# Turning the query packs in other steps of a decoder block, and masking the mixing weights on GpSimd

## The chip, the cores and the metric

The kernel runs on one core of one Trainium2 chip. The metric is the device time of the program in microseconds, the median of three runs. The profile is of one execution of its own; its times are given in us from the first instruction.

## The reference

The block takes `x` (512 positions of 1024 channels) through a normalisation and one input projection, whose columns are cut into `a_u`, `a_v`, attention `q`, `k`, `v`, indexer `q`, `k` and weights, and two gates. Branch A mixes positions in chunks of 128 by a lower-triangular matrix for each of eight groups; branch B is sparse attention with a partial rotary embedding on the first 32 channels of each head. Then come projections, gates, and a SwiGLU layer.

```python
h = rms_norm(x, norm1_g) * (1.0 + scale1) + shift1
a_u, a_v, q, k, v, qi, ki, wi, g_a, g_b = jnp.split(h @ w_in, split_points, axis=-1)

# chunked_gmlp(gelu(a_u), gelu(a_v), ...)
v = layer_norm(v, ln_g, ln_b).reshape(bsz, n, CHUNK, A_GROUPS, A_GROUP_DIM)
mask = jnp.tril(jnp.ones((CHUNK, CHUNK), dtype=w_s.dtype))
mixed = jnp.einsum('gts,bnsgc->bntgc', w_s * mask, v) + b_s.T[None, None, :, :, None]
y_a = u * mixed.reshape(bsz, s, A_WIDTH)

# partial_rope(q, pos, ROT_DIM) on 32 of 128 channels of each head
rot = jnp.concatenate([x1 * cos - x2 * sin, x2 * cos + x1 * sin], axis=-1)

merged = sigmoid(g_a) * (y_a @ w_proj_a) + sigmoid(g_b) * (y_b @ w_proj_b)
x = x + gate1 * (merged @ w_out)
```

## The kernel before

Every large product is made of three matmuls, high times high, high times low and low times high, where a float32 operand is split into a rounded high part and the rest, its low part. Weights come in chunks of 128x1024, in the order of a list. For each chunk the SyncE queue issues the load, ScalarE copies the high part (line 163), and VectorE or GpSimd subtracts it from the raw chunk to get the low part (line 167). `get` prepares a chunk two chunks ahead of the one whose matmuls are issued (24 of them, lines 107 to 109). All engines run their instructions in the order in which the program was written, so what is written earlier on an engine's queue stands ahead, waiting or not. The buffers of high and low parts are three each.

Three stages matter here. In the stage of `a_v` the loop over `s` goes through fourteen products (two halves of seven, a Strassen scheme), and the table `VT` says what else is issued at each step: weight splits, and steps of the packs below. Then `opt_b` runs over the eight chunks of `a_u`, and after them over pairs of chunks of gate A and projection A in turn, 24 chunks in all. I number them 0 to 23. Before each of them `au_tasks` is called, which counts the same number as its step `s`; after each `au_post` is called. The low parts of chunks 0 to 4 are VectorE's, those of chunks 5 to 23 nearly all GpSimd's.

- `ln_v` and `ln_v2` normalise `gelu(a_v)`: statistics in the last a_v steps and step 0, a power on GpSimd for the reciprocal root, then two operations of 128x1024 for each of four blocks on VectorE (lines 1139 and 1140), two blocks in step 1 and two in step 2.
- `mix_mm` (line 1153) multiplies `vg` with the masked mixing weights `wmT`: product 0 after chunk 3, 1 and 2 after chunk 4, 3 to 7 after chunks 5 to 9. `mix_ev` evacuates a product in the step that follows: VectorE adds the bias `bsb` and multiplies by `u`, ScalarE makes the high part of `y`, VectorE the low part. Chunks 10 and 11, of projection A, are the first to read `y`.
- `ws_mask` multiplies `wmT` by a triangle of ones, `triu`, which SyncE loads early from a constant; `load_ws` and `load_bs` load `wmT` and `bsb` from GpSimd's queue. In step 2 the program holds, in this order, the q4 turn, the mask, the bias load, and then the norms.
- `run_bg` puts operations of the search for the largest 128 scores (lines 856 and 860) between the others on VectorE.

The rotary embedding of `q` and `k` goes through packs (class `Packed`). `gather` writes the 32 rotated rows of each head to DRAM, `fetch` reads them back into a tile of 128 partitions, twice with the halves exchanged, `turn` does three VectorE operations with the table `tab_q`, `put` writes the result to DRAM, and `scatter` reads it back to its place. All these transfers are issued from GpSimd: `gather`, `fetch` and `scatter` are four issues each for a query pack, `put` one. There are three packs: `k`, `q0` (heads 0 to 3) and `q4` (heads 4 to 7). The first consumer of a turned query is `at_split` in step 20. All packs are fetched into the tile `S2_4`, which is needed for a part of `y` later. The bias tile `bsb` has the place of the table, `G3`, so its load waits for the last turn that reads the table.

Of the kernel before, what the change touches and what calls it, by code (L numbers as in the profile page):

```python
# [9 lines left out]
F32 = mybir.dt.float32  # L10
# [3 lines left out]
OP = mybir.AluOpType  # L14
AX = mybir.AxisListType

S = 512
# [40 lines left out]
@with_exitstack  # L58
def block_kernel(ctx: ExitStack, tc: tile.TileContext, x, x_t, w_in,
                 gmlp_ln_g, gmlp_ln_b, gmlp_w_s, gmlp_b_s, w_proj_a, w_proj_b,  # L60
                 w_out, w_ffn_in, w_ffn_out, final_norm_g, small, consts, c_row, w_shsc, out):
    nc = tc.nc
    T, V, A, P, SY = nc.tensor, nc.vector, nc.scalar, nc.gpsimd, nc.sync
    ctx.enter_context(tc.manual_schedule())
# [6 lines left out]
    x, out = x[0], out[0]  # L71
# [14 lines left out]
    def at_line(pool, tag, dims, dt, name, off=0):  # L86

        n = math.prod(dims)
        pad = 256 if tag == "E6" else (256 - HOME[tag]) % 256 or 192 if tag in HOME else 0
        t = pool.tile([128, n + pad // 4], dt, name=name, tag=tag, bufs=1)  # L90
        o = (off - HOME.get(tag, 0)) % 256 // 4
        letters = "abcd"[:len(dims)]
        return t[:, o:o + n].rearrange(f"p ({' '.join(letters)}) -> p {' '.join(letters)}",
                                       **dict(zip(letters[1:], dims[1:])))
# [505 lines left out]
    for kt in range(8):  # L600
        hi, lo = chunk[W1[kt]]
        V.tensor_sub(hT[kt][1], hfs[kt], f(hT[kt][0]))
        ensure(W1M[FIRST[kt]])
        if kt < 7:
            ensure(W1[kt + 1])
        wl = [(hi[:, 0, m * 128:(m + 1) * 128], lo[:, 0, m * 128:(m + 1) * 128]) for m in range(6)]
        hh, hl = hT[kt]
        kw = dict(skip_group_check=True)
        for m in range(6):
            T.matmul(outs[m], wl[m][0], hh, start=kt == 0, stop=False, **kw)  # L610
        for m in range(6):
            T.matmul(outs[m], wl[m][1], hh, start=False, stop=False, **kw)
        for m in range(6):
            T.matmul(outs[m], wl[m][0], hl, start=False, stop=kt == 7, **kw)
        if kt < 7:
            if kt < 5:
                low_w1(kt + 1)
            else:
                stream[W1[kt + 1]]["do"]()
            for k in (kt + 2,) if 0 < kt < 4 else (6, 7) if kt == 4 else ():  # L620
                row_scale(k)
            run_chain(kt == 1)
            ensure(W1M[BEHIND[kt]])
            stage_E(kt + 1)
        else:
            ensure(W_Q[0][1])
        if kt in (1, 2):
            A.activation(csb[:, (kt - 1) * 512:kt * 512], pc[:, (kt - 1) * 512:kt * 512], AF.Copy)
        if kt == 3:
            sines()  # L630
        if kt == 4:
            triu = mid.tile([128, 2, 128], F32, name="triu", tag="ql", bufs=2)[:, 0]
            SY.dma_start(triu, consts)
            for b in range(4):
                table_dma("q", b)
            for b in range(1, 4):
                table_dma("i", b)
            table_dma("i", 0)
            table_spread()
# [21 lines left out]
    class Packed:  # L661
# [14 lines left out]
                    P.dma_start(self.rows_of(0, 2 * self.rows, j, h), t[16 * h:16 * h + 16])  # L676

        def fetch(self):
            t = at_line(base, "S2_4", (2, S), F32, "pk")
            self.a, self.b = t[:, 0], t[:, 1]  # L680
            for o, flip in ((self.a, 0), (self.b, 1)):
                for h in range(2):
                    k = self.rows * (h ^ flip)
                    src = self.d[0][k:k + self.rows]
                    if self.rows < 64:
                        src = src[None].to_broadcast([2, 32, S])
                    P.dma_start(o[64 * h:64 * h + 64], src)
# [333 lines left out]
    late = {}  # L1021
# [8 lines left out]
        P.dma_start(late["wmT"], gmlp_w_s)  # L1030

    def load_bs():
        late["bsb"] = mid.tile([128, 8, 128], F32, name="bsb", tag="G3", bufs=1)
        P.dma_start(late["bsb"], bass.AP(tensor=gmlp_b_s.tensor, offset=gmlp_b_s.offset,
                                         ap=[[0, 128], [128, 8], [1, 128]]))

    def ws_mask():
        V.tensor_tensor(late["wmT"], late["wmT"], triu[:, None, :].to_broadcast([128, 8, 128]), op=OP.mult)

    for _ in range(16):  # L1040
        bg.append((1.4, topk_max))
# [34 lines left out]
    def av_add(k, op, src):  # L1076
        op(AV[k], AV[k], kept[src])

    pq0, pkk, pq4 = packs["q0"], packs["k"], Packed("q4", qf[2:])
    VT = {0: [lambda: av_sum(0, "T2"), lambda: av_w(0, "T2"), lambda: av_issue(1, "T1", "B11"), pq0.gather],  # L1080
          1: [lambda: av_w(0, "B21")],
          2: [lambda: av_w(0, "T3"), lambda: av_sum(0, "T4"), lambda: av_acc(1, "T1")],
          3: [lambda: av_w(0, "B22"), pkk.turn, pq4.gather],
          4: [lambda: av_w(0, "T4"), lambda: av_issue(1, "B21", "T3", "B22")],
          5: [lambda: av_w(1, "B11"), pkk.put],
          6: [lambda: av_w(1, "T1"), lambda: av_acc(1, "T3"), lambda: issue(W_AU[0][0])],
          7: [lambda: av_sum(1, "T2"), lambda: av_w(1, "T2"), pkk.scatter, pq0.fetch],
          8: [lambda: av_w(1, "B21")],
          9: [lambda: av_w(1, "T3"), lambda: av_sum(1, "T4"), pq0.turn],
          10: [lambda: av_w(1, "B22"), load_ln],  # L1090
          11: [lambda: av_w(1, "T4"), lambda: issue(W_AU[0][1]), lambda: ln_v(0, 0), pq0.put],
          12: [lambda: ensure(W_AU[0][0]), lambda: ln_v(1, 0), lambda: ln_v(2, 0), load_ws, pq0.scatter, pq4.fetch],
          13: [lambda: ensure(W_AU[0][1]), lambda: ln_v(3, 0), lambda: k_b(0)]}

    def av_post(g, p):
        if p == 0:
# [68 lines left out]
    austep = [0, 0]  # L1165
    AT = {3: [0], 4: [1, 2], 5: [3], 6: [4], 7: [5], 8: [6], 9: [7]}

    def au_post():
        for m in AT.get(austep[1], []):
            mix_mm(m)  # L1170
        austep[1] += 1

    def au_tasks():
        s = austep[0]
        austep[0] += 1
        if s == 0:
            k_b(1)
        if s == 2:
            pq4.turn()
            ws_mask()  # L1180
            load_bs()
        if s in (4, 5):
            (pq4.put, pq4.scatter)[s - 4]()
        if s == 0:
            for tk in range(4):
                ln_v(tk, 1)
            rstd(rva, mva[:, :, 1], 4, 1.0)
            run_bg(0.8)
        elif s == 1:
            ln_v2(0)  # L1190
            ln_v2(1)
        elif s == 2:
            ln_v2(2)
            ln_v2(3)
        for m in AT.get(s - 1, []):
            mix_ev(m)
        if s > 2:
            run_bg(1.6 if s < 8 else 2.0)
        if s in (20, 21):
            at_split(s - 20)  # L1200
# [976 lines left out]
    for tk in range(2):  # L2177
# [26 lines left out]


_INS = ["x", "x_t", "w_in", "gmlp_ln_g", "gmlp_ln_b", "gmlp_w_s", "gmlp_b_s",
        "w_proj_a", "w_proj_b", "w_out", "w_ffn_in", "w_ffn_out", "final_norm_g", "small", "consts",
        "c_row", "w_shsc"]
_OUTS = [((1, 512, 1024), "float32")]


def _constants():
    import numpy as np
    return np.triu(np.ones((128, 128))).astype(np.float32)


def _freqs():
# [44 lines left out]
```

## Time and profile before

| what | value |
|---|---|
| median of 3 runs | 790.44 us (789.35 to 790.44) |
| the profiled execution's own time | 789.18 us |
| its span, first to last instruction | 787.5 us |
| mean granted clock of TensorE | 0.994 |
| TensorE busy | 771.8 us, 98% |
| VectorE busy | 667.9 us, 85% |
| ScalarE busy | 440.0 us, 56% |
| GpSimd busy | 191.7 us, 24% |

PE is TensorE's matmuls, PEld its weight loads, DVE VectorE, ACT ScalarE, POOL GpSimd and SP SyncE. A row of a timeline gives the start, the duration and, in brackets, how long the engine was idle before it and what ended that. Instructions overlap a little at their ends, so the distance between two starts says more of the cost than a duration. A matmul's duration has the length of the pipeline in it. The granted clock is the share of full speed (2.4 GHz) that TensorE had; its lower level is 1.2 GHz.

### The profile page before, as it was taken

The page shows a single profiled execution, that of the slowest core. Times are in us where ns is not written, and L with a number is a line of the kernel's source. Part 1 is how long each engine was busy: PE and PEld are TensorE (multiplying, and loading weights), DVE is VectorE, ACT ScalarE, POOL GpSimd, SP SyncE. Part 2 cuts the span into 40 slices and gives each one's busy share as a digit, 9 for nine tenths or more (in the row PEclk, how much of TensorE's full clock was granted, in tenths as well). Part 3 has the DMA queues.
Part 4 walks back from the last instruction along what each step waited for, and adds up shares of the span by engine and source line. Part 5 has one row for each costly group of instructions (what it writes and reads, how often), then busy time and mean ns, then how long its engine had stood idle before and what let it go on. Part 6 is the DMA issues. An engine that isn't in the chain of part 4 may idle for free.

```text
span 787.5 us, 12682 instructions
## 1 busy us (share of the span) xinstructions
PE 771.8 (98%) x4723; PEld 692.4 (88%) x4723; DVE 667.9 (85%) x1115; ACT 440.0 (56%) x775; POOL 191.7 (24%) x268
## 2 busy tenths in 40 slices
PE   8999999989999999999999999999999999999996
PEld 6899899867888888998888899999999999888885
DVE  7889778998898559987697878989999888998886
ACT  6665557522232336666536577655566666676653
POOL 4872212323354411100010000313131223000002
PEclk9999999999999999999999999999999999999998
DMA  9967655732346558717681603889897977567662
GB/s 352 415 188 191 157 149 144 241 121 93 107 161 211 187 192 218 208 56 271 213 263 28 214 1 104 246 240 302 237 283 218 278 216 194 161 195 203 214 216 107
DMA packets 54656, 153.49 MB, mean 195 GB/s; under 512 B 15585, under 2 KB 16353, under 8 KB 54594
## 3 DMA queue, kind: packets, MB, share of 16 engines
q1 hardware_dynamic: 41696, 115.40, 43.6%
q0 software_dynamic: 12320, 36.32, 19.2%
q8 instruction: 37, 0.61, 0.3%
q10 hardware_dynamic: 578, 0.95, 0.3%
q14 instruction: 25, 0.20, 0.1%
HBM read 146.35 MB, written 28.71 MB: 222 GB/s over the span
## 4 chain that ended last, share of the span: by engine, by line
PE 76%; DVE 2%; issue 0%; ACT 0%; POOLq 0%; POOL 0%; DVEq 0%
PE R L107 8%; PE R L109 8%; PE R L108 8%; PE pb L108 7%; PE pb L107 7%; PE pb L109 6%; PE pfo L109 4%; PE pfo L107 4%; PE pfo L108 4%; PE pgb L107 2%; PE pgb L108 2%; PE pgb L109 2%; PE po L107 2%; PE po L108 2%; PE po L109 2%; PE pf L107 1%
## 5 line engine op out<-in xcount | busy, mean ns | idle before, releaser
L163 ACT ACTIVATE hi<-raw 128x1024 fp32r<-128x1024 f32 (+4 forms) x98 | 98.7, 1010 | 88.6 <-PE pb L108 29.5
L167 DVE TENSOR_TENSOR lo<-raw,hi 128x1024 fp32r<-128x1024 f32 (+2 forms) x71 | 82.9, 1168 | 22.3 <-ACT hi L163 22.1
L107 PE MATMUL pb<-h,hi 128*128 128x512 f32 (+1 forms) x192 | 74.1, 386 | 0.0
L108 PE MATMUL pb<-h,hi 128*128 128x512 f32 (+1 forms) x192 | 73.5, 383 | 0.0
L109 PE MATMUL pb<-h,lo 128*128 128x512 f32 (+1 forms) x192 | 73.3, 382 | 0.0
L167 POOL TENSOR_TENSOR lo<-raw,hi 128x1024 fp32r<-128x1024 f32 x19 | 46.0, 2425 | 64.1 <-ACT hi L163 60.1
L108 PE MATMUL pfo<-lo,za 128*128 128x512 f32 (+1 forms) x144 | 55.2, 383 | 0.0
L109 PE MATMUL pfo<-hi,za 128*128 128x512 f32 (+1 forms) x144 | 55.2, 383 | 0.0
L107 PE MATMUL pfo<-hi,za 128*128 128x512 f32 (+1 forms) x144 | 55.2, 383 | 0.0
L254 DVE CUSTOM_DVE_ANT_0 mraw<-mraw,csb,cols 128x1024 f32<-128x1024 f32 x27 | 37.8, 1399 | 18.6 <-DMA mraw<-in_w_shsc_dram 18.5
L387 POOL COPY sm<-sm 128x1 f32<-128x1 f32 x36 | 26.9, 751 | 94.1 <-ACT sm L386 94.1
L107 PE MATMUL R<-tb,hi 128*128 128x256 f32 x160 | 44.2, 276 | 0.0
L108 PE MATMUL R<-tb,hi 128*128 128x256 f32 x160 | 44.2, 276 | 0.0
L109 PE MATMUL R<-tb,lo 128*128 128x256 f32 x160 | 44.2, 276 | 0.0
L107 PE MATMUL R<-tb,sx 128*128 128x256 f32 x160 | 44.2, 276 | 0.0
L108 PE MATMUL R<-tb,sx 128*128 128x256 f32 x160 | 44.2, 276 | 0.0
L109 PE MATMUL R<-tb,sx 128*128 128x256 f32 x160 | 44.2, 276 | 0.0
L109 PEld LDWEIGHTS pb<-h,lo 128*128 128x128 f32 x192 | 36.3, 189 | 6.6 <-DVE lo L167 0.4
L107 PEld LDWEIGHTS pb<-h,hi 128*128 128x128 f32 x192 | 36.4, 190 | 6.0
L108 PEld LDWEIGHTS pb<-h,hi 128*128 128x128 f32 x192 | 36.4, 189 | 6.0
L367 POOL DMA_DIRECT2D wsum<-in_w_ffn_out_dram x24 | 19.6, 823 | 66.6 <-DMA wsum<-wsum 39.2
L108 PEld LDWEIGHTS pfo<-lo,za 128*128 128x128 f32 x144 | 27.1, 188 | 5.3
(419 smaller groups left out, 2666.9 us busy)
## 6 DMA issues: line engine op xcount, KB each, us to landing
raw<-in_w_ffn_in_dram SPq DMA_DIRECT2D x44, 512.0 KB
raw<-in_w_in_dram SPq DMA_DIRECT2D x38, 512.0 KB
wsum<-in_w_ffn_out_dram POOLq DMA_DIRECT2D x30, 512.0 KB, 7.1
mraw<-in_w_shsc_dram SPq DMA_DIRECT2D x27, 512.0 KB
raw<-wsum SPq DMA_DIRECT2D x20, 512.0 KB
s<-in_w_shsc_dram SPq DMA_DIRECT2D x14, 512.0 KB
raw<-in_w_ffn_out_dram SPq DMA_DIRECT2D x13, 512.0 KB
wsum<-wsum POOLq DMA_DIRECT2D x10, 512.0 KB, 5.8
```

The lines of the kernel that those rows point to most:

```text
L107: T.matmul(o, wh, rh, start=start, stop=False, **kw)
L108: T.matmul(o, wh, rlo, start=False, stop=False, **kw)
L109: T.matmul(o, wlo, rh, start=False, stop=stop, **kw)
L163: A.activation(hi[:, :m], e["raw"][:, :m], AF.Copy)
L167: e["lo"].tensor_sub(lo[:, :m], e["raw"][:, :m], f(hi[:, :m]))
L254: V.tensor_tensor_reduce(out=raw[:, c], in0=raw[:, c], in1=(csb if s > 1 else pc)[:, c], scale=scale, scalar=sums.pop(0), op0=OP.mult, op1 ...
L367: P.dma_start(wsum_at(n, c), src, max_dma_last_dim=4096, accum_op=OP.add)
L387: P.tensor_copy(t, t)
```

## The change

The two query packs are turned later. Before, the steps of `q0` were spread over the a_v loop and `q4` was gathered in its fourth step, fetched near its end, turned in step 2 of `au_tasks`, put in step 4 and scattered in step 5. Now both gathers are at the start of a_v, and the rest stands in a table `PT` for the steps of `au_tasks`: `q0` is fetched in step 4, turned in 7, put in 9 and scattered in 11; `q4` is fetched in 11, turned in 13, put in 15 and scattered in 16. Their tile is now `G0`, where the norm's gain `lng` lies until step 2. The steps of the `k` pack stay.

The triangle is no longer loaded. `ws_mask` is an affine select on GpSimd, which fills the other triangle of each group's 128x128 block with zero, in the last a_v step. The bias is loaded in the step before that, into the tile `L`, which holds a low part that the last but one product of a_v still reads.

```diff
         if kt == 4:
-            triu = mid.tile([128, 2, 128], F32, name="triu", tag="ql", bufs=2)[:, 0]
-            SY.dma_start(triu, consts)
             for b in range(4):
                 table_dma("q", b)
...
         def fetch(self):
-            t = at_line(base, "S2_4", (2, S), F32, "pk")
+            t = at_line(base, "S2_4", (2, S), F32, "pk") if self.rows < 64 else mid.tile(
+                [128, 2, S], F32, name="pk", tag="G0", bufs=1)
             self.a, self.b = t[:, 0], t[:, 1]
...
     def load_bs():
-        late["bsb"] = mid.tile([128, 8, 128], F32, name="bsb", tag="G3", bufs=1)
+        late["bsb"] = vmid.tile([128, 1024], F32, name="bsb", tag="L", bufs=1).rearrange("p (a n) -> p a n", a=8)
         P.dma_start(late["bsb"], bass.AP(tensor=gmlp_b_s.tensor, offset=gmlp_b_s.offset,
                                          ap=[[0, 128], [128, 8], [1, 128]]))
 
     def ws_mask():
-        V.tensor_tensor(late["wmT"], late["wmT"], triu[:, None, :].to_broadcast([128, 8, 128]), op=OP.mult)
+        P.affine_select(out=late["wmT"], in_=late["wmT"], pattern=[[0, 8], [1, 128]], compare_op=OP.is_ge, fill=0.0,
+                        base=0, channel_multiplier=-1)
...
-    VT = {0: [lambda: av_sum(0, "T2"), lambda: av_w(0, "T2"), lambda: av_issue(1, "T1", "B11"), pq0.gather],
+    VT = {0: [lambda: av_sum(0, "T2"), lambda: av_w(0, "T2"), lambda: av_issue(1, "T1", "B11"), pq0.gather, pq4.gather],
...
-          3: [lambda: av_w(0, "B22"), pkk.turn, pq4.gather],
+          3: [lambda: av_w(0, "B22"), pkk.turn],
...
-          7: [lambda: av_sum(1, "T2"), lambda: av_w(1, "T2"), pkk.scatter, pq0.fetch],
+          7: [lambda: av_sum(1, "T2"), lambda: av_w(1, "T2"), pkk.scatter],
           8: [lambda: av_w(1, "B21")],
-          9: [lambda: av_w(1, "T3"), lambda: av_sum(1, "T4"), pq0.turn],
+          9: [lambda: av_w(1, "T3"), lambda: av_sum(1, "T4")],
           10: [lambda: av_w(1, "B22"), load_ln],
-          11: [lambda: av_w(1, "T4"), lambda: issue(W_AU[0][1]), lambda: ln_v(0, 0), pq0.put],
-          12: [lambda: ensure(W_AU[0][0]), lambda: ln_v(1, 0), lambda: ln_v(2, 0), load_ws, pq0.scatter, pq4.fetch],
-          13: [lambda: ensure(W_AU[0][1]), lambda: ln_v(3, 0), lambda: k_b(0)]}
+          11: [lambda: av_w(1, "T4"), lambda: issue(W_AU[0][1]), lambda: ln_v(0, 0)],
+          12: [lambda: ensure(W_AU[0][0]), lambda: ln_v(1, 0), lambda: ln_v(2, 0), load_ws, load_bs],
+          13: [lambda: ensure(W_AU[0][1]), lambda: ln_v(3, 0), lambda: k_b(0), ws_mask]}
...
+    PT = {4: [pq0.fetch], 7: [pq0.turn], 9: [pq0.put], 11: [pq0.scatter, pq4.fetch], 13: [pq4.turn], 15: [pq4.put],
+          16: [pq4.scatter]}
...
         if s == 0:
             k_b(1)
-        if s == 2:
-            pq4.turn()
-            ws_mask()
-            load_bs()
-        if s in (4, 5):
-            (pq4.put, pq4.scatter)[s - 4]()
+        for fn in PT.get(s, []):
+            fn()
         if s == 0:
```

The argument `consts`, its array of ones and its entry in the list of inputs are dropped as well.

## Rows read from the trace of the kernel before

**Rows 1.** The page's first part: busy us, share of the span, instructions of each engine.

```profile
PE 771.8 (98%) x4723; PEld 692.4 (88%) x4723; DVE 667.9 (85%) x1115; ACT 440.0 (56%) x775; POOL 191.7 (24%) x268
```

**Rows 2.** TensorE's waits, 100 to 260 us: waiter, releaser: us, times, longest us.

```profile
PE mix L1153 <- DVE vg L1140: 3.8, 2, 2.0
PE pav L107 <- DVE pav L1077: 1.4, 1, 1.4
```

**Rows 3.** Stretches of the span: busy us (instructions) by engine, granted clock, DMA.

```profile
140.00:150.00 10.00, 8.62 (x73) 8.42 (x72) 9.90 (x18) 4.71 (x7) 3.97 (x7) 1.00 0.81 284
172.80:178.40 5.60, 1.42 (x7) 0.82 (x6) 5.53 (x6) 0.78 (x2) 0.00 (x0) 0.95 0.51 146
178.40:181.50 3.10, 3.09 (x9) 2.52 (x10) 3.10 (x8) 0.00 (x0) 0.00 (x0) 0.54 0.27 73
182.00:236.00 54.00, 54.00 (x268) 45.72 (x267) 47.64 (x107) 18.13 (x24) 24.03 (x13) 1.00 0.38 124
```

**Rows 4.** TensorE's timeline: start us, duration us, line, operation, tiles [idle before <-releaser].

```profile
172.64 0.39 PE L109 MATMUL pb<-h,lo 128*128 128x512 f32 x1
...
178.41 0.80 PE L1153 MATMUL mix<-wmT,vg 128*128 128x128 f32 x2 [2.03 <-DVE vg L1140]
...
181.44 0.39 PE L107 MATMUL pb<-h,hi 128*128 128x512 f32 x1
...
218.17 1.05 PE L1153 MATMUL mix<-wmT,vg 128*128 128x128 f32 x8
...
229.96 0.39 PE L107 MATMUL pb<-h,hi 128*128 128x512 f32 x1
...
240.84 0.39 PE L107 MATMUL pb<-y,hi 128*128 128x512 f32 x1
```

**Rows 5.** VectorE's timeline, same columns, a_v's last products to the first mixing product.

```profile
142.67 1.31 DVE L433 TENSOR_TENSOR lo<-avr,hi 128x1024 fp32r<-128x1024 f32 x1
...
150.38 1.21 DVE L167 TENSOR_TENSOR lo<-raw,hi 128x1024 fp32r<-128x1024 f32 x1
...
166.48 1.22 DVE L167 TENSOR_TENSOR lo<-raw,hi 128x1024 fp32r<-128x1024 f32 x1
167.61 0.68 DVE L690 TENSOR_TENSOR pk<-pk,tab_q 128x512 f32<-128x512 f32 x1
...
169.54 3.78 DVE L1038 TENSOR_TENSOR wmT<-wmT,triu 128x1024 f32<-128x1024 f32 x1
173.25 1.27 DVE L1139 SCALAR_TENSOR_TENSOR vg<-vg,mva,lng 128x1024 f32<-128x1024 f32 x1
...
177.07 1.28 DVE L1140 SCALAR_TENSOR_TENSOR vg<-vg,sm,lnb 128x1024 f32<-128x1024 f32 x1
```

**Rows 6.** GpSimd's timeline, same columns, 100 to 240 us.

```profile
141.69 1.21 POOL L849 TENSOR_SCALAR_AFFINE_SELECT sco<-sco 128x128 f32<-128x128 f32 x1 [2.26 <-DVE sco L843]
...
150.36 2.08 POOL L687 DMA_DIRECT2D pk<-pkq  x4
...
169.84 2.40 POOL L167 TENSOR_TENSOR lo<-raw,hi 128x1024 fp32r<-128x1024 f32 x1
...
225.89 4.77 POOL L167 TENSOR_TENSOR lo<-raw,hi 128x1024 fp32r<-128x1024 f32 x2 [4.47 <-ACT hi L163]
```

**Rows 7.** ScalarE's timeline, same columns, around a_v's end and chunk 3.

```profile
141.07 1.06 ACT L432 ACTIVATE hi<-avr 128x1024 fp32r<-128x1024 f32 x1 [1.33 <-PE pav L109]
...
167.38 1.06 ACT L163 ACTIVATE hi<-raw 128x1024 fp32r<-128x1024 f32 x1 [3.67 <-PE pb L108]
```

**Rows 8.** GpSimd's groups by shape: busy us, mean ns of one | idle before.

```profile
L369 POOL DMA_DIRECT2D wsum<-in_w_ffn_out_dram x12 | 8.8, 945 | 0.9 <-issue 0.9
...
L420 POOL TENSOR_SCALAR_AFFINE_SELECT ident<-ident 128x128 f32<-128x128 f32 x2 | 0.6, 294 | 0.1
```

**Rows 9.** The tile wmT: the request of its load and its landing.

```profile
L1030 POOL DMA_DIRECT2D wmT<-in_gmlp_w_s_dram x1: 535/535/535, 144.3 to 144.3; - x1
...
DMA to landing us min/median/max: 5.3/5.3/5.3
```

More of the change, by code (lines that the diff above doesn't have):

```diff
@@ L60, in block_kernel @@
                  gmlp_ln_g, gmlp_ln_b, gmlp_w_s, gmlp_b_s, w_proj_a, w_proj_b,
-                 w_out, w_ffn_in, w_ffn_out, final_norm_g, small, consts, c_row, w_shsc, out):
+                 w_out, w_ffn_in, w_ffn_out, final_norm_g, small, c_row, w_shsc, out):
     nc = tc.nc
@@ L2206 @@
 _INS = ["x", "x_t", "w_in", "gmlp_ln_g", "gmlp_ln_b", "gmlp_w_s", "gmlp_b_s",
-        "w_proj_a", "w_proj_b", "w_out", "w_ffn_in", "w_ffn_out", "final_norm_g", "small", "consts",
+        "w_proj_a", "w_proj_b", "w_out", "w_ffn_in", "w_ffn_out", "final_norm_g", "small",
         "c_row", "w_shsc"]
 _OUTS = [((1, 512, 1024), "float32")]
-def _constants():
-    import numpy as np
-    return np.triu(np.ones((128, 128))).astype(np.float32)
 def _freqs():
@@ L2233 @@
     given = dict(inputs)
-    given["consts"] = _constants()
     col = lambda a: _np.asarray(a).reshape(-1, 128).T
```

## The prediction

> **What bounds the kernel now.** I read the page first: TensorE is busy 98% of the span [rows 1], so an edit to work of the other engines shows only where TensorE waits or runs at its lower clock. The list of TensorE's waits between 100 and 260 us comes next, because that stretch holds everything the diff touches. It has two entries of size: 3.8 us at the first mixing product, for `vg` from VectorE, and 1.4 us near the end of the a_v stage, for an addition of VectorE [rows 2]. The stretch table shows what the first one costs beyond the wait: between 172.8 and 178.4 us TensorE has 1.42 us of work, and after it the granted clock is 0.54, which is nearly all at 1.2 GHz instead of 2.4 [rows 3]. TensorE's timeline gives the whole price. Its last matmul of chunk 3 starts at 172.64 and the pitch at full speed is 0.227 us (48 matmuls from 229.96 to 240.84), so it is free at 172.87; full pitch is back at 181.44 [rows 4]. In between it does eight mixing matmuls of 128 columns (eight of them took 1.05 us later, at full clock) and six of 512 (1.36), 2.4 us of work in 8.57 us. **6.2 us** are lost here: that is the most that this place can give.
>
> What is late there is VectorE's order [rows 5]. It runs without a gap from 166.48 on: a low part, three operations of the q4 pack's turn, the mask product on `wmT`, then the last two norms, whose final operation starts at 177.07 and lasts 1.28; TensorE goes on at 178.41. The mask is the odd one. It takes 3.78 us where a VectorE subtraction of as many elements takes 1.22. GpSimd's subtraction runs from 169.84 for 2.40 us [rows 6], all inside it. So I read it as 1.2 us of work and 2.4 to 2.5 us in which VectorE stood still while GpSimd read two operands from SBUF.
>
> **What leaves VectorE before the first mixing product.** The turn of q4 goes: 167.61 to 169.54, 1.93 us. The mask goes: 169.54 to 173.25 by the next start, 3.71 us. In the a_v stage the turn of q0 goes too, another 1.93, but not all of it counts. The next low part starts at 142.67, and its high part is ready on ScalarE only at 141.07 + 1.06 = 142.13 [rows 7], so 0.54 us is gained there, and the addition behind it, for which TensorE waited, comes as much earlier. Sum: 0.54 + 1.93 + 3.71 = **6.18 us**.
>
> **What comes in.** First, GpSimd's subtraction does not go away with the mask. Before, it stood in GpSimd's queue behind the bias load, which waited for the q4 turn to free its tile. Now the bias load is ahead of all that, and the subtraction starts when its high part is done: 167.38 + 1.06 on ScalarE [rows 7], 167.9 with the shift of 0.54. There VectorE is in the norms, which read two SBUF tiles as the mask did. If nothing holds it, VectorE's stop moves from the mask to the norms: bounds 0 and 2.5 us, and I take **2.35**, as the one row that shows such a meeting has it. The Trainium skill (SBUF — State Buffer, section Who interferes with whom) states that a VectorE operation with two SBUF inputs and a GpSimd operation that reads SBUF exclude one another for a whole instruction, by order of issue. The rows agree on the size, but there VectorE's operation began 0.30 us before GpSimd's and was still the one that stood. By that rule in its plain form the norm already running would go first and GpSimd next, which is the same sum; if VectorE kept the port from one norm to the next, the sum would be that of the first rival.
>
> Second, the mask on GpSimd. `wmT` is asked for at 144.3 and lands 5.3 us later [rows 9]; the request comes some 0.5 us sooner, so the select can start near 149.1. The price of 128x1024 isn't in the trace. Two clean 128x128 selects took 0.29 each [rows 8], so eight times that, 2.3 us, bounds it above; below, it can't be much under 1 us, for GpSimd's two-input subtraction of the same shape takes 2.40 and a select has one input. Near the middle, 1.3 to 1.6, it ends at about 150.5. A 128x128 select that met a VectorE subtraction took 1.21 instead of 0.29 [rows 6], so such meetings cost whoever is second. The low part that VectorE starts at 150.38 [rows 5] would start at 149.84 and stand some **0.5 us** (bounds 0 and 1.6).
>
> What waits behind these on GpSimd? The bias load waits for the last but one product of a_v, which still reads its new tile; behind it stands the select, whose data lands after that product ends anyway, and then the small operations of the norm, which wait for statistics that VectorE has only in chunk 1. That wait hides both. The four gathers of q4 move to the start of a_v, where GpSimd is idle, and the load of the triangle disappears from SyncE's queue early in the kernel. I cost these at nothing: neither queue has a TensorE wait behind it in the list.
>
> VectorE's chain to the first mixing product is then 6.18 - 2.35 - 0.5 = 3.3 us shorter, and TensorE goes on near 175.1. It waits about 2 us in one piece instead of 4.2 in three. The stretch with the 1.4 us wait kept a granted clock of 1.00 [rows 3], so I expect the lower clock not to come. VectorE's low part of chunk 4, 1.2 us, stands right behind the norms and holds TensorE at its third matmul some 0.5 us. Chunk 4 then starts, in effect, at 175.8, against 181.44 - 1.36 = 180.1: TensorE is 4.3 us ahead.
>
> **What is given back.** VectorE is only 3.3 us ahead, 1.0 less than TensorE, and from there to the last evacuation it has no idle time but the round trips to ScalarE (47.64 us busy of 54) [rows 3]. There the change puts the q0 turn, 1.93 us, at step 7, ahead of the evacuation of the fifth mixing product. From there VectorE is 3.33 - 1.93 = 1.4 us ahead of before. ScalarE's high part of chunk 12 stands behind the last evacuation, which VectorE feeds, and GpSimd's low parts of chunks 12 and 13 follow it, from 225.89 on, in 4.77 us [rows 6]. So low part 12 ends at 225.89 + 2.40 - 1.4 = 226.9. Chunk 12 on TensorE would start at 229.96 - 4.3 = 225.7, and its third matmul is the first that needs the low part: a stall of about 0.8.
>
> Then the queue that these moves crowd: step 11 puts the scatter of q0 and the fetch of q4 on GpSimd, ahead of low part 13. Four such issues take 2.08 us [rows 6], eight 4.1. Low part 13, which followed low part 12 at once before, ends at 226.9 + 4.1 + 2.4 = 233.4. Chunk 13 needs it at its third matmul, with 22 pitches to go: 233.5 + 22 x 0.227 = 238.5 for the start of chunk 14, against 240.84 before [rows 4]. **2.35 us remain.** Whatever TensorE wins at the mixing product beyond this, it waits for here. Nothing later eats it: low part 14 ends about 235.8, and chunk 14 needs it at 239. The put of step 15 and the four issues of step 16 meet a queue that holds one subtraction of 2.4 us in each chunk of 5.4, and the q4 turn of step 13 comes after the last evacuation.
>
> The profiled execution took 789.18 us, 1.68 more than its span, and 1.26 less than the median of the runs shown, 790.44. So 786.8 for an execution like the profiled one, and on the scale of the median 790.44 - 2.35 = **788.1 us**.
>
> **The rivals.** *VectorE isn't stopped in the norms* (the GpSimd subtraction waits until they are through; chunk 5, the second after, is the first to need it). Then the chain is 2.35 to 2.85 us shorter, low part 13 ends as much earlier, and the gain is 4.7 to 5.2: 785.2 to 785.7. For it: only one row shows VectorE stopped so. Against: its size fits to a tenth.
>
> *The gain is eaten.* The select takes its 2.3 us or starts late, VectorE stands 1.5 us instead of 0.5 and the q0 turn meets a GpSimd subtraction: another microsecond or more. The gain falls to 0.3 to 1.3 us, 789.1 to 790.1. For it: VectorE has no reserve from step 4 to 11, so every stop there reaches low part 13.
>
> *Slower: GpSimd's queue at step 11.* The eight issues come to more than 4.1 us. At 0.95 each, as twelve weight copies between DRAM tensors took [rows 8], they are 7.6 and low part 13 ends at 236.9: chunk 14 starts at 242.0, 1.1 us later than before, 791.6. No change is reached at 6.5 us for the eight, 0.81 each; 0.2% slower at 8.1. Against it: issues of these very copies took 0.52 before.
>
> **The numbers.** 0.2% of 790 us, 1.6 us, is about what a measurement of this kernel can tell from no change. Chances: forecast (gain 1.4 to 4) 0.48, VectorE not stopped 0.20, eaten 0.20, GpSimd's queue 0.12. A small part of the forecast's chance lies within 0.2% and a small part of the last rival's too: faster 0.67, same 0.23, slower 0.10. The range, **784.8 to 790.3**, takes in the first rival and nearly all of the second; the forecast's own is 786.4 to 789.1.
>
> **What would show it.** TensorE's waits: the entry at the mixing product about 2 us in one piece, no stretch at 1.2 GHz after it. On VectorE no mask; one of the norms at 3.5 us instead of 1.28, beside a GpSimd subtraction near 168. GpSimd: a select of 1 to 2.3 us near 149; eight issues in a row before low part 13, and TensorE waiting for that low part at chunk 13, near 233. A gain above 4 us with norms all at 1.28 is the first rival; no wait of TensorE at chunks 12 and 13 means that I have VectorE too late from step 7 on. I'd be wrong altogether if the lower clock came back.

## The result and the profile after

The changed kernel takes **795.32 us** (median of 5 runs, 792.26 to 796.77); the kernel before, run beside it, 790.44. The ratio is **1.0055 [1.0029, 1.008]** (worked out from all executions, so it can differ a little from the quotient of two medians; the brackets are a 95% interval): it is slower by 4.3 us, where 788.1 was predicted and 790.3 was the top of the range. The profiled execution took 796.77 us, with a span of 795.0.

Up to chunk 14 the profile looks as the prediction drew it. First VectorE, with the columns of [rows 5], then GpSimd, with those of [rows 6]:

```profile
168.44 3.30 DVE L1140 SCALAR_TENSOR_TENSOR vg<-vg,sm,lnb 128x1024 f32<-128x1024 f32 x1
```

```profile
148.82 1.09 POOL L1037 TENSOR_SCALAR_AFFINE_SELECT wmT<-wmT 128x1024 f32<-128x1024 f32 x1
...
168.03 2.63 POOL L167 TENSOR_TENSOR lo<-raw,hi 128x1024 fp32r<-128x1024 f32 x1 [8.11 <-ACT hi L163]
...
223.72 2.39 POOL L167 TENSOR_TENSOR lo<-raw,hi 128x1024 fp32r<-128x1024 f32 x1 [4.48 <-ACT hi L163]
226.05 2.04 POOL L699 DMA_DIRECT2D qf<-pkq  x4
228.08 2.08 POOL L686 DMA_DIRECT2D pk<-pkq  x4
230.15 4.76 POOL L167 TENSOR_TENSOR lo<-raw,hi 128x1024 fp32r<-128x1024 f32 x2
...
242.31 2.53 POOL L167 TENSOR_TENSOR lo<-raw,hi 128x1024 fp32r<-128x1024 f32 x1 [4.04 <-ACT hi L163]
...
247.62 2.38 POOL L167 TENSOR_TENSOR lo<-raw,hi 128x1024 fp32r<-128x1024 f32 x1 [1.37 <-ACT hi L163]
```

The mask is gone from VectorE, and the stop has moved from it to a norm: 3.30 us instead of 1.28, beside GpSimd's subtraction of 168.03. The select takes 1.09 us. The eight DMA issues of step 11 (226.05 and 228.08) stand between low part 12 (223.72) and low parts 13 and 14 (4.76 us from 230.15). Now TensorE's timeline and, in the second fence, its waits from 140 to 400 us (columns as in [rows 4] and [rows 2]):

```profile
174.31 0.49 PE L1153 MATMUL mix<-wmT,vg 128*128 128x128 f32 x2 [1.10 <-DVE vg L1140]
...
226.16 0.50 PE L109 MATMUL pb<-h,lo 128*128 128x512 f32 x1 [0.59 <-POOL lo L167]
...
232.62 0.50 PE L109 MATMUL pb<-h,lo 128*128 128x512 f32 x1 [0.72 <-POOL lo L167]
...
237.74 0.39 PE L107 MATMUL pb<-y,hi 128*128 128x512 f32 x1
...
263.43 0.77 PE L107 MATMUL pb<-y,hi 128*128 128x512 f32 x1 [3.77 <-DVE part L1247]
...
264.42 0.63 PE L109 MATMUL pb<-y,lo 128*128 128x512 f32 x1
264.85 0.63 PE L107 MATMUL pb<-y,hi 128*128 128x512 f32 x1
...
319.44 0.50 PE L107 MATMUL pgb<-h,hi 128*128 128x512 f32 x1 [2.01 <-ACT gb L1396]
```

```profile
PE pb L107 <- DVE part L1247: 3.8, 1, 3.8
PE pgb L107 <- ACT gb L1396: 2.0, 1, 2.0
...
PE mix L1153 <- DVE vg L1140: 1.1, 1, 1.1
```

TensorE waits 1.10 us at the mixing product instead of 3.8 in two pieces [rows 2], with no lower clock behind it, and starts chunk 14 at 237.74 instead of 240.84 [rows 4]: **3.10 us ahead**. Then two waits come that the kernel before doesn't have: 3.77 us at 263.43, where chunk 18 needs the PSUM banks that VectorE's product `part` (L1247) empties, and 2.01 us at 319.44, for the evacuation `gb` of the first gate-B group on ScalarE. After the first the pitch is 0.42 us (264.42 to 264.85) instead of 0.227. The stretches, after and then before (columns as in [rows 3]), show the same: a granted clock of 0.91 and 0.96, part of it at 1.2 GHz, where before had 1.00 throughout:

```profile
262.00:300.00 38.00, 36.57 (x148) 29.98 (x149) 24.02 (x49) 12.78 (x19) 11.95 (x5) 0.91 0.57 194
300.00:340.00 40.00, 37.99 (x195) 32.74 (x194) 36.48 (x87) 27.22 (x61) 7.98 (x16) 0.96 0.81 211
```

```profile
262.00:300.00 38.00, 38.00 (x169) 31.34 (x168) 20.59 (x46) 15.59 (x26) 9.57 (x4) 1.00 0.53 186
300.00:340.00 40.00, 40.00 (x235) 35.38 (x234) 36.60 (x93) 27.84 (x66) 7.84 (x16) 1.00 0.72 192
```

So the lead of 3.10 is spent by the first wait (3.77), and the lower clock and the second wait bring the rest of the 7.5 us by which this execution's span is longer.

What was late at both places is on VectorE. It does 15 **dots** there (L254: a 128x1024 row block of the modulation weights, landed in the tile `mraw`, times a vector, with a sum). `mraw` is one tile: when a dot ends, SyncE asks for the next block, and behind that for the next block of weights; the next dot waits for the landing. Dots 4 to 8 and the first softmax operation, which stands behind the 15th, before and then after:

```profile
228.47 3.27 DVE L254 CUSTOM_DVE_ANT_0 mraw<-mraw,csb,cols 128x1024 f32<-128x1024 f32 x1
...
235.22 1.29 DVE L254 CUSTOM_DVE_ANT_0 mraw<-mraw,csb,cols 128x1024 f32<-128x1024 f32 x1 [0.49 <-DMA mraw<-in_w_shsc_dram]
...
240.79 1.29 DVE L254 CUSTOM_DVE_ANT_0 mraw<-mraw,csb,cols 128x1024 f32<-128x1024 f32 x1
...
245.65 1.29 DVE L254 CUSTOM_DVE_ANT_0 mraw<-mraw,csb,cols 128x1024 f32<-128x1024 f32 x1 [0.58 <-DMA mraw<-in_w_shsc_dram]
...
250.60 1.28 DVE L254 CUSTOM_DVE_ANT_0 mraw<-mraw,csb,cols 128x1024 f32<-128x1024 f32 x1 [0.68 <-DMA mraw<-in_w_shsc_dram]
...
288.95 0.68 DVE L1286 CUSTOM_DVE_ANT_0 pt<-qk,sco 128x512 f32<-128x512 f32 x1
```

```profile
226.31 1.27 DVE L254 CUSTOM_DVE_ANT_0 mraw<-mraw,csb,cols 128x1024 f32<-128x1024 f32 x1
...
231.84 4.16 DVE L254 CUSTOM_DVE_ANT_0 mraw<-mraw,csb,cols 128x1024 f32<-128x1024 f32 x1 [1.28 <-DMA mraw<-in_w_shsc_dram]
...
240.10 1.26 DVE L254 CUSTOM_DVE_ANT_0 mraw<-mraw,csb,cols 128x1024 f32<-128x1024 f32 x1
...
241.30 0.68 DVE L689 TENSOR_TENSOR pk<-pk,tab_q 128x512 f32<-128x512 f32 x1
241.90 0.68 DVE L690 TENSOR_TENSOR pk<-pk,tab_q 128x512 f32<-128x512 f32 x1
242.62 2.77 DVE L691 TENSOR_TENSOR pk<-pk 128x512 f32<-128x512 f32 x1
...
248.28 2.81 DVE L254 CUSTOM_DVE_ANT_0 mraw<-mraw,csb,cols 128x1024 f32<-128x1024 f32 x1
...
255.76 1.28 DVE L254 CUSTOM_DVE_ANT_0 mraw<-mraw,csb,cols 128x1024 f32<-128x1024 f32 x1 [1.69 <-DMA mraw<-in_w_shsc_dram]
...
294.70 0.69 DVE L1285 CUSTOM_DVE_ANT_0 pt<-qk,sco 128x512 f32<-128x512 f32 x1
```

Dot 4 is 2.2 us earlier than before, dot 7 is 2.6 later, dot 8 is 5.2 later, and the softmax 5.75. Four things stand between them. Dot 5 takes 4.16 us, beside low parts 13 and 14, which step 11's issues have pushed there. The turn of q4 (241.30 to 245.31) takes 4.0 us: 1.93 of work and 2.1 in which its last operation stands beside GpSimd's subtraction of 242.31 (such a stop is called a lock below). Dot 7 takes 2.81, beside that of 247.62. The block of dot 8 comes 1.0 us slower, beside the four issues of q4's scatter from 249.95 on: 4.64 us from its request (251.12) to the waiting dot, 3.63 before. And the chain can't catch up. The tile `mraw` before, first the dots (least, median, longest in ns), then what VectorE's idle time ended with (us, times):

```profile
L254 DVE CUSTOM_DVE_ANT_0 mraw<-mraw,csb,cols x15: 1258/1284/3270, 207.8 to 287.4; 128x1024 f32<-128x1024 f32 x15
...
  DMA mraw<-in_w_shsc_dram: 17.1, 9
```

Nine of the 15 dots wait for their block already in the kernel before, 17.1 us in all. From dot 5 on their pitch, some 5 us, is that of one landing tile: request, landing, dot. Late dots also delay the weights, whose requests stand behind those for `mraw` on SyncE: that for chunk 18 goes out at 251.54 here and at 247.39 before, and ScalarE's high part of it starts at 258.10 instead of 251.92.

How much TensorE can gain is decided at the second of its waits, which I call gate B. The first softmax stands right behind dot 15 on VectorE, and on ScalarE the evacuation `gb` stands behind the softmax's later steps. That evacuation and the matmul that needs its bank, before and then after (the matmul after is shown above, at 319.44):

```profile
313.06 1.06 ACT L1397 ACTIVATE gb<-pgb 128x512 f32<-128x512 f32 x2
```

```profile
313.68 0.50 PE L107 MATMUL pgb<-h,hi 128*128 128x512 f32 x1
```

```profile
318.81 1.06 ACT L1396 ACTIVATE gb<-pgb 128x512 f32<-128x512 f32 x2
```

The matmul starts 0.62 to 0.63 us behind the evacuation in both, and 26.28 us behind the last dot (287.40 and 293.16). So in this execution the kernel before was held there too, by 0.13 us only (the matmul ahead starts at 313.32, and the pitch is 0.227). What TensorE gains at the front can't pass this place unless the last dots come earlier as well.

### The profile page after: what moved, and what is told of

It reads as the page before. It is cut to its first block, busy times and chain, and to the rows that moved or that the text cites. A ratio compares the mean times of both kernels' runs of the same rounds, so it can differ in the third digit from the quotient of the medians.

```text
span 795.0 us, 12688 instructions
## 1 busy us (share of the span) xinstructions
PE 775.9 (98%) x4723; PEld 695.0 (87%) x4723; DVE 674.7 (85%) x1114; ACT 440.1 (55%) x775; POOL 193.0 (24%) x269
## 4 chain that ended last, share of the span: by engine, by line
PE 58%; DVE 13%; DMA 4%; issue 2%; ACT 2%; POOLq 0%; POOL 0%; DVEq 0%; ACTq 0%
PE R L107 8%; PE R L108 8%; PE R L109 8%; PE pfo L109 4%; PE pfo L108 4%; PE pfo L107 4%; DMA mraw<-in_w_shsc_dram 4%; DVE mraw L254 2%; DVE sco L859 2%; PE pb L108 2%; PE pb L109 2%; PE pb L107 2%; DVE m L855 2%; PE po L107 2%; PE po L109 2%
## 5 line engine op out<-in xcount | busy, mean ns | idle before, releaser
L254 DVE CUSTOM_DVE_ANT_0 mraw<-mraw,csb,cols 128x1024 f32<-128x1024 f32 x27 | 39.8, 1474 | 17.1 <-DMA mraw<-in_w_shsc_dram 17.1
```

The source lines that it names most:

```text
L254: V.tensor_tensor_reduce(out=raw[:, c], in0=raw[:, c], in1=(csb if s > 1 else pc)[:, c], scale=scale, scalar=sums.pop(0), op0=OP.mult, op1 ...
```

## The experiments

**T1**, formed on this reading: the loss comes from VectorE's chain of dots, which has hardly any reserve from the fifth dot on; the turn of step 13 and the crowd of step 11 make it late. **R1**: the transfers of the moved packs slow the loads of that chain. **R2**: the select, its tile or the norms locked by GpSimd are what costs. Every ratio below is to the kernel before, run beside it on the same chip; 0.001 is 0.8 us.

| run | median us | ratio | dot 4 | dot 6 | dot 8 | dot 15 | gate B |
|---|---|---|---|---|---|---|---|
| before | 790.44 | | 228.47 | 240.79 | 250.60 | 287.40 | 313.68 |
| changed | 795.32 | 1.0055 [1.0029, 1.008] | 226.31 | 240.10 | 255.76 | 293.16 | 319.44 |
| mask alone | 788.56 | 0.9981 [0.9969, 0.9992] | 228.36 | 240.95 | 251.18 | 289.02 | 315.30 |
| packs alone | 796.38 | 1.0073 [1.0061, 1.0085] | 227.34 | 241.18 | 256.74 | 293.38 | 319.67 |
| q4's turn at 18 | 791.44 | 1.0013 [1.0004, 1.0022] | 226.48 | 240.29 | 250.48 | 289.56 | 315.85 |
| q4's fetch at 13, turn at 18 | 790.50 | 0.9991 [0.9978, 1.0003] | 226.35 | 238.76 | 249.06 | 287.89 | 314.16 |
| without q4's turn | 791.08 | 1.0002 [0.999, 1.0013] | 225.78 | 239.60 | 249.41 | 286.53 | 312.81 |
| before, a turn more at 13 | 794.15 | 1.0032 [1.0015, 1.0048] | 228.31 | 240.68 | 251.78 | 288.52 | 314.79 |
| before, a turn more at 7 | 791.20 | 1.0000 [0.999, 1.001] | 230.13 | 242.41 | 252.37 | 289.05 | 315.34 |
| before, two landing tiles | 790.15 | 0.9997 [0.9987, 1.0006] | 229.03 | 240.55 | 249.78 | 280.60 | 314.29 |
| changed, two landing tiles | 789.87 | 0.9998 [0.9981, 1.0014] | 226.50 | 242.65 | 254.65 | 284.75 | 312.75 |
| q0 before, q4 at 13 to 20 | 789.66 | 0.9991 [0.9982, 1.0] | 224.78 | 238.13 | 248.31 | 286.34 | 312.62 |
| q0 before, q4 at 4 to 11 | 787.80 | 0.9974 [0.996, 0.9988] | 228.30 | 240.08 | 250.29 | 285.90 | 312.19 |
| the same, two landing tiles | **786.38** | **0.9948 [0.9936, 0.996]** | 227.66 | 241.78 | 251.64 | 283.31 | 311.25 |

(The last five columns are starts in the profiled execution, in us: of four dots and of the matmul at gate B.)

Gate B less dot 15 is 26.27 to 26.29 us in every run with one landing tile, and 28 to 34 with two. So with one tile the chain decides where TensorE stands there, in all eleven.

Each execution also has an offset of its own that it had before any of the moved steps. ScalarE's high part at 84.48 us in the kernel before comes 1.4 us later in the trace of mask alone and 1.2 later with q4 at 4 to 11; it comes 0.6 later in the first and the last of the runs with two tiles, 0.4 earlier without q4's turn and with q4 at 13 to 20, and within 0.3 us in the others. Single starts of two runs are to be compared less these.

**Mask alone, packs alone.** The first leaves the packs where they were (the bias load moves with the mask), the second puts the triangle's product back on VectorE:

```diff
 mask alone, on the kernel before
-        V.tensor_tensor(late["wmT"], late["wmT"], triu[:, None, :].to_broadcast([128, 8, 128]), op=OP.mult)
+        P.affine_select(out=late["wmT"], in_=late["wmT"], pattern=[[0, 8], [1, 128]], ...)
 packs alone, on the changed kernel: these two lines the other way round, the product at step 2
```

> Only the mask (select on GpSimd, bias in the other tile) is changed; both query packs are turned and sent where the kernel before has them. Theory T1 (the loss is the chain of the index dots on VectorE, made late in a_u's chunks 12 to 16 by the pack's DMA issues of step 11 and by q4's turn of step 13): nothing is added to that stretch, so the gain at the first mixing product stays. The 3.71 us of the mask leave VectorE's chain; the lock of low part 5 may give back up to 2.35, so the wait of 3.8 us there becomes 0.1 to 2.5 us, without the low clock: 3.5 to 6 us faster than before, 784.5 to 787 us, and the dot of before's 240.79 us begins at least 2 us earlier. Rival R2 (the select, its tile or the norms locked by GpSimd are what costs): 790 us or more. Rival R1 (transfers of the moved packs slow the loads of the dots' chain) says the same as T1.

> Only the packs are moved (as in the changed kernel); the mask is VectorE's product at step 2 again. T1 and R1: the front gains what q4's turn took from VectorE's chain (1.93 us, so a wait of about 2 us at the first mixing product), and the stretch of chunks 12 to 16 loses as the changed kernel does: dots 5 to 5.8 us late from the ninth on, chunk 18 stalled by 3 to 4 us, 793 to 798 us. R2: 786 to 790 us, because the mask's part of the change is undone.

Mask alone is 1.5 us faster, packs alone 5.8 slower, and the sum is the changed kernel's 4.3 (each of the three to 1 or 2 us). R2 falls: the packs bring all of the loss. But mask alone gains less than the 3.5 to 6 us expected. The trace, of an execution of 790.62 us (its 12 lie between 787.38 and 791.26), shows the reason, on VectorE and on GpSimd:

```profile
167.92 1.22 DVE L167 TENSOR_TENSOR lo<-raw,hi 128x1024 fp32r<-128x1024 f32 x1
...
170.38 2.77 DVE L690 TENSOR_TENSOR pk<-pk 128x512 f32<-128x512 f32 x1
```

```profile
169.95 2.65 POOL L167 TENSOR_TENSOR lo<-raw,hi 128x1024 fp32r<-128x1024 f32 x1 [8.09 <-ACT hi L163]
```

With q4's turn still at step 2, its last operation is the one that stands beside GpSimd's subtraction (2.77 us instead of 0.69). So of the mask's 3.71 us 2.08 come back and 1.63 are won. TensorE still waits 2.8 us in two pieces, and the lower clock comes, against the expectation: 0.77 was granted from 172 to 182 us. The low part that started at 166.48 [rows 5] starts at 167.92, which is this execution's offset and nothing more. Nor does dot 6 come at least 2 us sooner, as expected: less the offset it is 1.3 sooner, and the last dot 0.2 later.

**The turn of step 13 and the crowd of step 11.**

```diff
 q4's turn at 18
-    PT = {..., 11: [pq0.scatter, pq4.fetch], 13: [pq4.turn], 15: [pq4.put], 16: [pq4.scatter]}
+    PT = {..., 11: [pq0.scatter, pq4.fetch], 18: [pq4.turn], 19: [pq4.put], 20: [pq4.scatter]}
 q4's fetch at 13, turn at 18
+    PT = {..., 11: [pq0.scatter], 13: [pq4.fetch], 18: [pq4.turn], 19: [pq4.put], 20: [pq4.scatter]}
 without q4's turn
+    PT = {..., 11: [pq0.scatter, pq4.fetch], 15: [pq4.put], 16: [pq4.scatter]}
```

> The changed kernel, with q4's turn, put and scatter at steps 18, 19 and 20 instead of 13, 15 and 16; its eight fetches stay at step 11. T1 in two halves. If the turn of step 13 is the greater half (1.93 us, and 2.1 us in its third operation's lock): the dots are 1 to 3 us late instead of 5 to 5.8, chunk 18 is stalled under 1 us, 787 to 791 us. If the crowd of step 11 (eight issues, low parts 13 and 14 pushed into the fifth dot: 2.9 us) is enough by itself: dots 4 us late or more, 792 to 796 us. If the turn alone matters: dots not late, 785 to 787.5 us. R1: the transfers of the fetch are unchanged, so 793 to 797 us.

> The changed kernel with q4's fetch at step 13, its turn at 18, put at 19 and scatter at 20: against the run with only the turn moved to 18, the four issues of the fetch leave step 11. T1: low part 13 is 2.1 us earlier, the stall of 0.7 us at chunk 13 goes; the locked dot becomes the fourth again (3.3 us instead of 4.2), the later dots are 1 to 2 us earlier: 789 to 790.7 us. Rival (the crowd costs nothing more, the chain is bound by q4's turn at 18 and by its loads): 791 to 792 us.

> The changed kernel without the three VectorE operations of q4's turn at step 13 (two heads' queries stay unrotated); its gathers, fetches, put and scatter stay where they are, so every transfer is kept. T1: the dots from the sixth on are 0 to 2 us late against before instead of 5 to 5.8; no stall at chunk 18; 789.5 to 791.5 us, like the run with the turn at 18 and up to 1 us better. R1 (the packs' transfers slow the loads of the chain): as the changed kernel, 794 us or more.

(q4's fetch is four issues, not eight; the eight of step 11 are q0's scatter and this fetch.) The first lies 0.4 us above the range for the turn as the greater half, the other two inside theirs. One detail failed: with the fetch at 13 the locked dot is still the fifth, with 2.33 us, and not the fourth. Moving the turn takes off 0.0042, or 3.3 us; leaving it out takes off 0.0053, or 4.2, with every transfer in its place. R1 falls with that as the main cause. It may have a share: blocks that are requested while a pack's transfers are under way (those of dots 5 and 8 in the changed kernel, others without the turn and with q4 at 13 to 20) take 4.2 to 5.2 us to the waiting dot, where the kernel before has 3.4 to 4.3. But with the turn at 18 one takes 5.0 (251.80 to 256.78) with no pack beside it, so the share isn't shown. The fetch at step 13 takes off another 0.0022, or 1.7 us (on another chip; the intervals just don't overlap), and the 0.7 us of gain that it leaves can't be told from none. Dot 8 starts at 249.1 to 250.5 in all three, instead of 255.76. The turn at 18 isn't free either. With the fetch still at 11, VectorE and then GpSimd:

```profile
271.81 2.79 DVE L254 CUSTOM_DVE_ANT_0 mraw<-mraw,csb,cols 128x1024 f32<-128x1024 f32 x1 [1.39 <-DMA mraw<-in_w_shsc_dram]
```

```profile
271.10 2.41 POOL L167 TENSOR_TENSOR lo<-raw,hi 128x1024 fp32r<-128x1024 f32 x1
```

The dot behind the turn (268.20 to 270.13) comes late enough to meet GpSimd's subtraction and takes 2.79 us, and TensorE waits 2.4 us for `ql` at its first scores. Nor is the turn all. Without it TensorE is 3.6 us ahead of before at chunk 14 (237.25), but the last dot is only 0.87 ahead, and at gate B TensorE waits 2.3 us and is 0.87 ahead too.

**A turn more in the kernel before.** The cost alone, without the change: three more operations of a turn's shape, at step 13 and at step 7.

```diff
+        if s == 13:
+            t = mid.tile([128, 2, S], F32, name="extra", tag="G0", bufs=1)
+            V.tensor_mul(t[:, 1], csb[:, :512], csb[:, 512:])
+            V.tensor_mul(t[:, 0], csb[:, :512], csb[:, 512:])
+            V.tensor_add(t[:, 0], t[:, 0], t[:, 1])
```

> The kernel before with three more VectorE operations of a turn's shape at step 13 (128x512, two inputs in SBUF, on a tile of their own); no transfer is added and nothing else is moved. T1: the chain of dots has no reserve, so 1.9 us of work, up to 4 us with a lock by GpSimd's low part, makes every later dot as late; TensorE, which has no gain from the front here, waits for it at chunk 18 and at the first gate-B evacuation: 792.5 to 796 us. Rival (the turn is only dear where the crowd of step 11 has made the chain late already): 790 to 791.5 us.

> The kernel before with the same three more VectorE operations as in the run with them at step 13 (128x512, two inputs in SBUF, a tile of their own), but at step 7. T1 (a turn is dear only in the chain of dots, from step 11 or so on): before, low part 12 lands 2.1 us ahead of the matmul of chunk 12 that needs it, which covers the 1.93 us; 790 to 791.5 us. Rival (a turn costs as much anywhere in a_u): 792.5 to 796 us, as the run at step 13 had (794.15).

At step 13 it costs 0.0032, 2.5 us; at step 7 nothing that can be told (interval 0.8 us to either side), though in its trace the dots are 1.7 us late to the end, TensorE waits 0.9 us at gate B and is 1.7 late there too. The two can be reconciled if the kernel before mostly has about a microsecond of reserve at gate B. The one trace of the kernel before is of a short execution (789.18 us). In the three other traces that keep its mixing product unchanged (a turn more at 13 and at 7, two landing tiles) TensorE loses 0.2 to 1.2 us more in the stretch behind it: a clock of 0.64 to 0.79 was granted there from 178 to 186 us, and 0.80 in before's. That is likely, not shown. One thing stays open: the profiled execution of step 13 was the shortest of its 12 (790.19 to 797.31). TensorE is 1.06 us late there already at chunk 14 (241.90), from that stretch, and 1.11 at gate B, as the last dot is. So in it the turn cost TensorE next to nothing, and its trace doesn't show where the 2.5 us lie. VectorE, then GpSimd, in it:

```profile
243.21 0.69 DVE L1186 TENSOR_TENSOR extra<-extra 128x512 f32<-128x512 f32 x1
```

```profile
243.72 2.45 POOL L167 TENSOR_TENSOR lo<-raw,hi 128x1024 fp32r<-128x1024 f32 x1 [3.66 <-ACT hi L163]
```

Here the turn's last operation began 0.5 us ahead of GpSimd's subtraction and took its 0.69; in the changed kernel it began 0.3 us behind one and took 2.77. That the longer executions are those with such a meeting is likely, not shown.

**Two landing tiles.**

```diff
                     add_m(*m, mid=mods is mm_ and mraw)
+                    if stream[-1]["mid"] == "A2":
+                        nmid[0] += 1
+                        if nmid[0] % 2 == 0 and nmid[0] < 16:
+                            stream[-1]["mid"] = "G1"
```

> The kernel before with the second landing tile alone. T1: TensorE has no wait after the first mixing product there, so an earlier chain brings nothing: 789.8 to 791 us, no difference that can be told. If it is over 1 us faster, the second tile helps by itself and the two runs of the changed kernels say less.

> The changed kernel with the second landing tile alone; the crowd of step 11 and the turn of step 13 stay. T1: the three long operations (4.16, 2.77, 2.81 us) remain in VectorE's order, but the loads no longer wait for them, so the lateness of 5 to 5.8 us is caught up at the following dots: the stall at chunk 18 under 1.5 us, the one at gate B under 0.5, 787.5 to 791 us. Rival R1 (transfers of the packs make the loads slow) or a bound on VectorE's own time: 793 us or more.

In the kernel before they bring nothing that can be told, though the last dot comes 6.8 us earlier: TensorE waited 0.13 us for the chain there. In the changed kernel they take off 0.0057, 4.5 us, with crowd and turn in place. That is T1's last link: the stops hurt because one landing tile lets none of them be caught up. The stops themselves are as long or longer; dot 5 now meets three subtractions, here on VectorE and then on GpSimd:

```profile
230.66 7.88 DVE L254 CUSTOM_DVE_ANT_0 mraw<-mraw,csb,cols 128x1024 f32<-128x1024 f32 x1
```

```profile
230.36 7.10 POOL L167 TENSOR_TENSOR lo<-raw,hi 128x1024 fp32r<-128x1024 f32 x3
```

**Versions meant to be faster.** The select stays; q0 goes as in the kernel before; q4 is sent as before and has its later steps in a_u:

```diff
+        for fn in {13: [pq4.fetch], 18: [pq4.turn], 19: [pq4.put], 20: [pq4.scatter]}.get(s, []):
 and, in the other two runs,
+        for fn in {4: [pq4.fetch], 7: [pq4.turn], 9: [pq4.put], 11: [pq4.scatter]}.get(s, []):
             fn()
```

> The select as in the changed kernel; q0 is sent, fetched and turned in a_v as before, q4 is sent as before but its fetch stands at step 13, its turn at 18, its put at 19 and its scatter at 20. T1: step 2 has neither turn nor mask, so the wait at the first mixing product is under 2 us, and no issue stands ahead of the low parts at step 11 nor a turn at 13; step 13's eight issues (4.1 us of GpSimd) stand behind the fifth dot. 3.5 to 6.5 us faster than before, 784 to 787 us. R1: q4's transfers still lie in chunks 13 to 20, beside the loads of the dots' chain, and cost as much as in the changed kernel: 789 us or more. A third way: the eight issues at step 13 push later low parts into later dots, by 2 to 3 us: 786.5 to 790 us.

> The select as in the changed kernel, q0 in a_v as before, and q4 in the place that the changed kernel gives q0: fetch at step 4, turn at 7, put at 9, scatter at 11. T1 (VectorE's chain of dots from the fifth on, with its one landing tile, is the bound; a turn costs there and little ahead of it): nothing stands in the chain, so the dots keep their lead of 2 to 2.5 us to the end (the run with q4 at step 18 had 2.2 until its turn), TensorE 3 to 3.5 ahead then waits up to 1 us for the first gate-B evacuation: 787.3 to 789 us. Rival (a turn costs its 1.93 us and a lock wherever it stands): as the run with q4 at step 18 or slower, 789.5 to 791.

> As the run with q4 at step 7, and every second landing tile of the dots' chain is another tile (A2 and G1 by turns), so that the request for one no longer waits for the dot before. T1: the waits of VectorE on these loads (0.6 to 4 us each from the fifth dot on) go or shrink, the requests for weights behind them on SyncE go out sooner, nothing is late at the first gate-B evacuation, and the front's gain arrives whole: 785 to 787.3 us. Rival: the landing tile isn't what binds (the loads are as late because their queue or DMA bandwidth is): same as with one tile, within 0.5 us.

With q4 at 13 to 20 the front's gain is the largest of all: dot 4 is 3.7 us early (3.3 less the offset), dot 8 2.3, dot 15 1.1. No dot is locked behind the four issues of step 13; it is the turn at 18 again, with a dot of 2.60 us behind it, and TensorE waits 1.1 us for `ql` and 2.2 for `gb`: 789.66, and not the 784 to 787 that T1 was taken to give. By its number alone this run fits R1 (789 or more) and the third way (786.5 to 790). The trace shows no lock in dots 5 to 9, and VectorE waits 15.9 us for `mraw` (17.1 before), which speaks against both as the main cause. I had counted nothing for a turn at 18. With the turn at 7 the run is 2.1 us faster than before (inside its range, though the dots' lead is not the steady 2 to 2.5 us expected but, less the offset, 1.4 us at dot 4 and 2.7 at dot 15), and with the second landing tile **4.1 us faster: 786.38 us**, the best here. VectorE's wait for `mraw` in this last run, and its stretch from 262 to 300 us:

```profile
DVE mraw L254 <- DMA mraw<-in_w_shsc_dram: 3.5, 3, 2.1
```

```profile
262.00:300.00 38.00, 38.00 (x169) 31.33 (x168) 31.18 (x58) 16.09 (x28) 10.87 (x7) 1.00 0.57 199
```

The wait is 3.5 us instead of the 17.1 above, and TensorE works through the stretch at full clock.

## Why the prediction was wrong

- *The wait at the mixing product*: right in kind. About 2 us in one piece was forecast and 1.10 came, with no lower clock behind it; TensorE goes on 4.1 us sooner (174.31) and not 3.3, since the stop in the norms added 2.0 us (2.35 taken) and the 0.5 us of the low part beside the select didn't come.
- *What comes in*: right, each a little dear. The norm that stops takes 3.30 us (3.5 forecast), the select 1.09 (1.3 to 1.6 taken).
- *What is given back*: right. The stalls at chunks 12 and 13 are 0.59 and 0.72 us (0.8 forecast for the first), the eight issues 4.12 (4.1), chunk 14 starts at 237.74 (238.5 forecast).
- **The step that failed** is the sentence "Nothing later eats it", and in it "the q4 turn of step 13 comes after the last evacuation". The turn was looked at only for the mixing products' evacuations and GpSimd's queue only for TensorE's low parts. Behind both stands the chain of dots, with nine waits for its one landing tile. There the turn costs 3.3 us (its move to 18) and the crowd of step 11 1.7 (the fetch at 13); together they make 4.3 us of loss out of 0.7 of gain. Most of the rest of the 3.1 us at chunk 14 is lost even without any turn of q4 (0.87 us are left at gate B): the premise that other engines' work shows only where TensorE waits or runs at its lower clock leaves out gate B, where TensorE in the kernel before is held by 0.13 us, too little for the list of waits. With the turn at step 7 and a second landing tile 4.1 us reach the end. Had the prediction listed VectorE's waits from 200 to 300 us as it listed TensorE's, the 17.1 us would have stood in the first line.
- *The rivals*: none was it. "Slower" was placed in GpSimd's queue at step 11 with issues dearer than shown; they cost what the row said, and their harm was to VectorE, through the low parts pushed into dot 5.
- "I'd be wrong altogether if the lower clock came back": it did, 90 us later, behind the wait at chunk 18.

## What to carry to other kernels

A stretch without TensorE waits has no spare by that alone: list the waits of the other engines there too. A chain that goes through one landing tile (request, landing, work, next request) runs at its own pitch and keeps what is put into it: here TensorE stood 26.28 us behind its last dot in eleven runs. The same turn six chunks earlier cost too little to measure in the median. So when work is moved to a later place, read at the new place what the engine waits for, and what its neighbours on the queue will be pushed into. A second landing tile gave nothing in the kernel before, 2.1 us behind a front that had been made shorter, and 4.5 where the chain had been made late. And when two traces are compared, take off the difference that they have ahead of the change, up to 1.4 us here.

## What the hardware showed

A VectorE operation with two inputs in SBUF that began while GpSimd subtracted ended about 1.1 us (for 128x1024) after GpSimd, whatever was due: 3.30, 2.81 and 4.16 us above instead of 1.27. The Trainium skill (SBUF — State Buffer, section Who interferes with whom) says that the one issued first holds the port for its whole instruction and the other blocks. The 0.69 us operation that began 0.5 us ahead of GpSimd agrees; the mask product, which began 0.30 us ahead and stood [rows 5, 6], doesn't. And over two and three subtractions in a row VectorE was not let in between: 4.16 us beside 4.76 us of two, and 7.88 beside 7.10 us of three, though the second and third came after the dot had begun. By order of issue the dot would have followed the first of them. The measurement decides: two or three low parts in a row on GpSimd can count as one block for such an operation. They don't always. With q4's turn at 18 a dot that began in the first of three (231.96) took 4.22 us and ended 1.1 us after the second, and the three took 8.10 us instead of 7.10: there the third one stood. What decides between the two is not shown.
